# A first product that takes x times g before the norm, and a normed x made while the product runs

## The chip, the cores and the metric

The kernel runs on one core of a Trainium2 chip, as one launch. The core's engines run side by side, each working through its own list of instructions in order: TensorE (PE in the profile; PEld is its load of the stationary operand), VectorE (DVE), ScalarE (ACT), GpSimd (POOL) and SyncE (SP), which issues nearly all transfers. Semaphores join them. The metric is the device time of one execution in microseconds; the time of the kernel before is the median of 3 runs, 882.23 us (881.98 to 883.07).

## The reference

Two layers, each a mixer block and an MLP, on x of 256 tokens by 1024 columns in float32. Only the start of a layer matters here:

```python
def rmsnorm(x, g):
    y = xf * lax.rsqrt(jnp.mean(xf * xf, axis=-1, keepdims=True) + EPS)
    return y * g

for l in range(DEPTH):                       # DEPTH = 2
    h = rmsnorm(x, norm_mix_g[l])
    proj = h @ w_in[l]                       # split: mqk, mv, mo, mi, mf, aq, ak, av, ga, gb
    ...                                      # mLSTM branch, window attention, output projection
    x = x + mixer_block(...)
    x = x + square(relu(rmsnorm(x, norm_mlp_g[l]) @ w_up[l])) @ w_down[l]
return rmsnorm(x, final_norm_g)
```

With r the reciprocal root of a token's mean square, h = (x g) r: r is one number per token (row), g one per column. A product with h's rows can therefore be taken with x g, and each row of the result multiplied by r afterwards.

## The kernel before, in words

**Products in three parts.** A float32 operand is split in a rounded part, hi, and the rest, lo = value - hi. A product is three matmuls: hi with hi, lo with hi, hi with lo (lines L220 to L222 in the helper `xs`, where 128 tokens are the rows of the result; L234 to L236 in `ws`, where the weight's columns are). A weight arrives in pieces of 128x1024 (512 KB) in one of four raw buffers. ScalarE casts the piece to hi (`pump_hi`, L152), VectorE subtracts (`pump_lo`, L127), and the subtraction frees the raw buffer, so the transfer of the piece four further on is issued right behind it, on SP (L89, L108, L109). There are seven pairs of hi and lo.

**Slots.** The program is a list of slots, one for each piece. For each slot are emitted, in this order: what `at` put there; hi of all pieces up to four ahead of the slot's own (`AHEAD`; the table `limits` lowers this at the start); what `at_late` put; lo of the same pieces with the next transfers; what `at_last` put; the slot's matmuls; what `after` put. This is the order of instructions on every engine; nothing moves later.

**The first product.** Slots 0 to 7 ("mv", pieces p0 to p7) compute the values mv: 256 tokens (two token tiles tt of 128) by 1024 columns in two halves hf, so four PSUM banks, each with 8 x 3 matmuls of 128x512, 12 matmuls in a slot, 96 in all. After slot 7 the four banks are copied to the tile vm (ScalarE L605 for hf 0, VectorE L603 for hf 1). Slots 8 to 11 ("kv", p8 to p11) compute the keys kk, values and gates of the attention in three banks that come out of those four; then follow the queries "aq" from slot 12 on. Up to the end all is of this kind.

**The start.** `setup_start` issues the loads: x, the gain row g, the pieces p0 to p3, then eleven small loads (`small_loads`, L393 to L399: gates' biases and sinks spread over 128 partitions, convolution weights), and lets TensorE run 26 + 16 + 8 matmuls on a block of zeros (`N_WARM`, L419, L425, L561). `first_norm` squares x (ScalarE L342, VectorE L344), makes r (VectorE L348, GpSimd L349), multiplies x by r (L534), transposes 128x128 blocks on TensorE (L539) and makes from the PSUM, with the factor g, the parts xh (ScalarE L543, four of 128x128 for half a token tile) and xl (VectorE L549). The first product goes by token tile in slots 0 to 3 (`head="t"`): slots 0 and 1 take tile 0 and the pieces p0 to p3, slots 2 and 3 tile 1; from slot 4 on a slot takes one piece and both tiles. `setup_cols` (slot 4) transposes the convolution rows and the relative bias; `setup_small` (slot 2) fills small constants.

## Time and profile before

| what | us |
|---|---|
| median of 3 runs | 882.23 |
| the profiled execution | 882.83 |
| its span, first to last instruction | 881.1 |
| busy: TensorE, VectorE, ScalarE | 867.6, 566.5, 468.8 |
| first matmul of the first product starts | 8.89 |
| first matmul of slot 5 starts | 27.27 |
| first matmul of the keys (slot 8) starts | 35.74 |
| mean granted clock of TensorE | 0.995 |

Outside the span lie 1.7 us of the profiled execution. Times in the timeline count from the span's start. A row of the timeline has start, length, engine, line, operation, tiles, and in brackets how long the engine had been idle and what released it. In a table by windows the columns are: window and its length, then busy time and number of instructions of PE, PEld, DVE, ACT and POOL, the granted clock (1.00 is full), the share of the DMA engines and GB/s. A group's row gives number, busy time, mean ns of one, and idle time ahead with its releaser. A row of the chain of waits is start, length, and what filled it.

### The profile page before, as it was taken

The numbers are of one execution on the slowest core, as the hardware profiler recorded it, in microseconds if no ns is written. First come the engines' busy times: TensorE is split into PE (matmuls) and PEld (weight loads), VectorE is DVE, ScalarE is ACT, GpSimd is POOL, SyncE is SP. The second block draws the span as 40 slices with busy tenths as digits, with TensorE's granted clock in tenths as the row PEclk, the third lists the DMA queues.
The fourth block names the chain that finished last, engine by engine and source line by source line (L and its number), as shares of the span: only waits on it lengthen the run. The fifth ranks groups of instructions, "written<-read, shape, count | busy, mean of one in ns | idle before, by whom it ended". The sixth has DMA issues, their size and how long they took to land.

```text
span 881.1 us, 15013 instructions
## 1 busy us (share of the span) xinstructions
PE 867.6 (98%) x5929; PEld 792.4 (90%) x5929; DVE 566.5 (64%) x897; ACT 468.8 (53%) x771; POOL 123.1 (14%) x164
## 2 busy tenths in 40 slices
PE   8999999999999999999999999999999999999996
PEld 6899879999989999998889998899998899999985
DVE  5758869666666654546474687776667764737363
ACT  5657866554355554544355567765634453636252
POOL 1361722120000000000001454122000000000000
PEclk9999999999999999999999999999999999999998
DMA  6875445445556737474655453454564466555521
GB/s 217 288 244 190 123 142 164 146 145 163 173 192 209 242 124 253 128 245 128 226 169 192 148 182 109 161 168 144 154 222 158 145 227 222 196 187 188 194 96 48
DMA packets 50711, 155.28 MB, mean 176 GB/s; under 512 B 7912, under 2 KB 10192, under 8 KB 50640
## 3 DMA queue, kind: packets, MB, share of 16 engines
q1 hardware_dynamic: 49456, 150.69, 52.6%
q0 software_dynamic: 896, 3.17, 1.1%
q8 instruction: 46, 0.75, 0.3%
q10 hardware_dynamic: 288, 0.46, 0.1%
q14 instruction: 25, 0.20, 0.1%
HBM read 153.23 MB, written 1.07 MB: 175 GB/s over the span
## 4 chain that ended last, share of the span: by engine, by line
PE 87%; DVE 5%; issue 2%; DMA 2%; ACT 2%; SPq 1%; POOL 1%; POOLq 0%; DVEq 0%; ACTq 0%
PE pa L220 11%; PE pa L221 11%; PE pa L222 11%; PE pa L235 11%; PE pa L234 11%; PE pa L236 11%; PE pb L235 5%; PE pb L234 5%; PE pb L236 5%; DMA raw<-in_w_in 2%; DVE lo L127 2%; PE pb L322 1%; PE pb L860 1%; PE pb L879 1%; PE pb L918 1%
## 5 line engine op out<-in xcount | busy, mean ns | idle before, releaser
L127 DVE TENSOR_TENSOR lo<-raw,hi 128x1024 fp32r<-128x1024 f32 (+1 forms) x276 | 331.5, 1224 | 136.0 <-ACT hi L152 133.5
L152 ACT CAST hi<-raw 128x1024 fp32r<-128x1024 f32 (+1 forms) x280 | 286.1, 1049 | 186.3 <-PE pa L222 49.7
L234 PE MATMUL pa<-xh,hi 128*128 128x256 f32 x864 | 246.6, 285 | 0.0
L235 PE MATMUL pa<-xl,hi 128*128 128x256 f32 x864 | 242.7, 281 | 0.0
L236 PE MATMUL pa<-xh,lo 128*128 128x256 f32 x864 | 241.6, 280 | 0.0
L234 PEld LDWEIGHTS pa<-xh,hi 128*128 128x128 f32 x864 | 162.6, 188 | 1.2 <-ACT vm L605 0.4
L235 PEld LDWEIGHTS pa<-xl,hi 128*128 128x128 f32 x864 | 163.1, 189 | 0.3
L236 PEld LDWEIGHTS pa<-xh,lo 128*128 128x128 f32 x864 | 162.8, 188 | 0.0
L220 PE MATMUL pa<-hi,xh 128*128 128x512 f32 (+1 forms) x384 | 150.5, 392 | 1.5 <-ACT xh L543 1.4
L221 PE MATMUL pa<-lo,xh 128*128 128x512 f32 (+1 forms) x384 | 148.4, 386 | 0.2 <-DVE lo L127 0.2
L222 PE MATMUL pa<-hi,xl 128*128 128x512 f32 (+1 forms) x384 | 148.3, 386 | 0.0
L234 PE MATMUL pb<-xh,hi 128*128 128x256 f32 x384 | 107.6, 280 | 0.0
L235 PE MATMUL pb<-xl,hi 128*128 128x256 f32 x384 | 107.6, 280 | 0.0
L236 PE MATMUL pb<-xh,lo 128*128 128x256 f32 x384 | 107.3, 280 | 0.0
L222 PEld LDWEIGHTS pa<-hi,xl 128*128 128x128 f32 x384 | 72.5, 189 | 15.6
L220 PEld LDWEIGHTS pa<-hi,xh 128*128 128x128 f32 x384 | 72.5, 189 | 14.8 <-ACT xh L543 1.6
L221 PEld LDWEIGHTS pa<-lo,xh 128*128 128x128 f32 x384 | 72.6, 189 | 13.9 <-DVE lo L127 0.6
L349 POOL TENSOR_TENSOR sm<-sm,mhalf 128x1 f32<-128x1 f32 x9 | 6.5, 725 | 499.8 <-DVE sm L348 499.8
L235 PEld LDWEIGHTS pb<-xl,hi 128*128 128x128 f32 x384 | 72.4, 188 | 1.7
L234 PEld LDWEIGHTS pb<-xh,hi 128*128 128x128 f32 x384 | 72.2, 188 | 1.8
L236 PEld LDWEIGHTS pb<-xh,lo 128*128 128x128 f32 x384 | 72.3, 188 | 0.0
L220 PE MATMUL pa<-hi,b 128*128 128x512 f32 x124 | 48.8, 394 | 0.0
(210 smaller groups left out, 979.2 us busy)
## 6 DMA issues: line engine op xcount, KB each, us to landing
raw<-in_w_in SPq DMA_DIRECT2D x104, 512.0 KB, 4.5
raw<-in_w_up SPq DMA_DIRECT2D x64, 512.0 KB, 4.7
raw<-in_w_down SPq DMA_DIRECT2D x64, 512.0 KB, 4.3
raw<-in_w_branch_a SPq DMA_DIRECT2D x16, 512.0 KB, 3.5
raw<-in_w_branch_m SPq DMA_DIRECT2D x16, 512.0 KB, 4.1
raw<-in_w_out SPq DMA_DIRECT2D x16, 512.0 KB, 4.5
b<-ed SPq DMA_DIRECT2D x4, 512.0 KB, 5.4
g<-in_mlstm_norm_g POOLq DMA_DIRECT2D x2, 512.0 KB, 6.1
```

Source lines behind the costliest of these rows:

```text
L127: nc.vector.tensor_tensor(lo[:, :n], raw[:, :n], hi[:, :n].bitcast(F32), op=ALU.subtract)
L152: nc.scalar.copy(hi[:, :n], raw[:, :n])
L220: nc.tensor.matmul(b, xh[:, kt, s], wh[:, c], start=first, stop=False)
L221: nc.tensor.matmul(b, xh[:, kt, s], wl[:, c], start=False, stop=False)
L222: nc.tensor.matmul(b, xl[:, kt, s], wh[:, c], start=False, stop=last)
L234: nc.tensor.matmul(o, wh[:, c], xh[:, kt, :], start=first and half == 0, stop=False, skip_group_check=True)
L235: nc.tensor.matmul(o, wh[:, c], xl[:, kt, :], start=False, stop=False, skip_group_check=True)
L236: nc.tensor.matmul(o, wl[:, c], xh[:, kt, :], start=False, stop=last, skip_group_check=True)
L322: nc.tensor.transpose(pt[:, j * P : (j + 1) * P], src[:, j * P : (j + 1) * P], ident)
L860: nc.tensor.transpose(tp[:, j * P : (j + 1) * P], L[:, j * P : (j + 1) * P], ident)
L879: nc.tensor.matmul(o, va[:, 0, vs], PT[:, 0:T], start=(h < h0 + 2), stop=False, skip_group_check=True)
L918: nc.tensor.matmul(pn[:, :257], W[:, tt * P : (tt + 1) * P], vm[:, 0, h, :], start=True, stop=(tt == 0))
```

## The change

Only the first layer's start is touched. Its parts:

1. **The first product takes x g.** x is transposed as it lands (TensorE L556), with no norm. For chunks 0 to 3 of each token tile hi and lo come straight from PSUM with the factor g (`hi4` ScalarE L570, `lo4` VectorE L576). For chunks 4 to 7 (`rest`, in slots 1 and 2) VectorE first writes x g (`times_g`, L562) and ScalarE and VectorE split it from there (L566, L580); `times_g` is also run for chunks 0 to 3 at the end of slot 1, since x g is needed later.
2. **r is applied when the banks are emptied**: the copies of slot 7 become a scaling by r (ScalarE L656, VectorE L654). The squares are taken in slots 2 and 3.
3. **The normed x for the keys** is made in slots 5 and 6: `rows` has TensorE spread r over partitions (L625, two matmuls) and ScalarE copy it (L628, the tile R); `normed(c)` multiplies four chunks of x g by R (VectorE L633, 128x1024) and splits them (ScalarE L323, VectorE L324).
4. **Order of slots 0 to 3**: by piece (`head="k"`), slot 0's units with hf 0 first, and p0 is loaded, cast (L139) and subtracted (L144) in halves. Limits of hi ahead are 1, 2, 3, 4, 5 for slots 0 to 4.
5. **Loads**: first the left halves of both token tiles, p0 in halves, p1, p2, the right halves, p3; the g row on ScalarE's queue; six small loads, of which a row of biases and sinks is spread by a matmul in `setup_cols` (L460), now in slot 5. `setup_small` moves to slot 8, its two copies to slot 10. `N_WARM` is 22, 6, 14.
6. **The keys take their PSUM bank first**, before the two banks of the values.

```diff
-    N_WARM = (26, 16, 8)
+    N_WARM = (22, 6, 14)
...
+        nc.scalar.dma_start(grow, norm_mix_g[0].rearrange("(k c) -> k c", c=P))
+        for tt in range(2):
+            nc.sync.dma_start(X[:, tt, 0:512], xv[:, tt, 0:512])
+        pump_dma(2)
+        pump_dma()
+        pump_dma()
+        for tt in range(2):
+            nc.sync.dma_start(X[:, tt, 512:], xv[:, tt, 512:])
+        pump_dma()
         small_loads()
...
+        def times_g(tt, hf):
+            nc.vector.tensor_tensor(xg[sl(tt, hf)], pts[tt, hf].rearrange("p (k t) -> p k t", k=4),
+                                    gcol[:, 4 * hf : 4 * hf + 4].unsqueeze(2).to_broadcast([P, 4, P]), op=ALU.mult)
+        def hi4(tt):
+            for j in range(4):
+                nc.scalar.activation(uh[:, j, tt * P : (tt + 1) * P], pts[tt, 0][:, j * P : (j + 1) * P], AF.Copy,
+                                     scale=gcol[:, j : j + 1])
...
+        hi4(0)
+        lo4(0)
+        pump_hi_part(0, 512)
         pump_lo_part(0, 512)
+        hi4(1)
+        lo4(1)
+        pump_hi_part(512, 1024)
         pump_lo_part(512, 1024)
         pump_lo_done()
         pump_hi(0, 1)
         pump_lo()
...
+        u = slots[nxt][0]
+        u[1], u[2] = u[2], u[1]
+        limits[nxt] = 1
+        for i in range(1, 5):
+            limits[nxt + i] = 1 + i
+        for tt in range(2):
+            slots[nxt + 1 + tt][0].insert(2, call(lambda tt=tt: rest(tt)))
+            at_last(nxt + 2 + tt, lambda tt=tt: norm(tt))
...
+        def rows():
+            pr = psB()
+            for tt in range(2):
+                nc.tensor.matmul(pr[:, tt * P : (tt + 1) * P], N[tt].r[:, 0:1].to_broadcast([P, P]), ident, start=True,
+                                 stop=True, skip_group_check=True)
+            S0["R"] = tmp()
+            nc.scalar.copy(S0["R"][:, 0:T], pr[:, 0:T])
+            st["hT"] = xT_tiles(xtag)
+        def normed(c):
+            s = (slice(None), slice(4 * c, 4 * c + 4), slice(None))
+            nc.vector.tensor_tensor(xg[s], xg[s], S0["R"][:, 0:T].unsqueeze(1).to_broadcast([P, 4, T]), op=ALU.mult)
+            evac_split(xg[s], st["hT"][0][s], st["hT"][1][s])
+        at(nxt + 5, rows)
+        at(nxt + 5, lambda: normed(0))
+        at(nxt + 6, lambda: normed(1))
+        for tt in range(2):
+            at_last(nxt + 1, lambda tt=tt: times_g(tt, 0))
...
-        s_mv = xs_group(st, "mv", "hT", w, MV0, head="t")
+        s_mv = xs_group(st, "mv", "hT" if l else "hU", w, MV0, head="t" if l else "k")
...
+            if l == 0:
+                r = S0["r"][tt]()
+                if hf:
+                    nc.vector.tensor_scalar(o, i, r, None, op0=ALU.mult)
+                else:
+                    nc.scalar.activation(o, i, AF.Copy, scale=r)
...
-        at(s_kv, lambda: st.update({("kv", 0): psA(), ("kv", 1): psA(), "kk": psA()}))
+        at(s_kv, lambda: st.update({"kk": psA(), ("kv", 0): psA(), ("kv", 1): psA()}))
...
-            at(s_mv + 2, setup_small)
-            at(s_mv + 4, setup_cols)
+            at(s_mv + 8, setup_small)
+            at(s_mv + 10, setup_copies)
+            at(s_mv + 5, setup_cols)
```

**How the order of instructions moves.** ScalarE, before, from hi of p8 (`hi_397`) to the emptying of the banks and the pieces behind it (`raw`: the piece as loaded, `pa`: a bank):

```order
L152 CAST hi_397<-raw_301 128x1040
L152 CAST hi_423<-raw_346 128x1040
L152 CAST hi_441<-raw_401 128x1040
L152 CAST hi_459<-raw_405 128x1040
L605 COPY vm<-pa_241 128x2x256
L605 COPY vm<-pa_243 128x2x256
```

ScalarE, now, from hi of p5 (`hi_314`): `tmp_370` is R, `xh_372` the hi part of the normed x.

```order
L162 CAST hi_314<-raw_207 128x1024
L628 COPY tmp_370<-pb_367 128x256
L323 CAST xh_372<-b_11_142 128x1024
L162 CAST hi_377<-raw_229 128x1024
L162 CAST hi_380<-raw_257 128x1024
L162 CAST hi_383<-raw_291 128x1040
L162 CAST hi_386<-raw_318 128x1040
L323 CAST xh_372<-b_11_142 128x1024
L162 CAST hi_418<-raw_390 128x1040
L162 CAST hi_436<-raw_394 128x1040
L656 ACTIVATE vm<-pa_209,sm_264 128x2x256
```

R and a cast of the normed x now stand ahead of hi of p6 to p9, and a second cast ahead of hi of p10 and p11 (`hi_436`), which the emptying of the banks follows.

VectorE, now, at the same place, from lo of p5 (`lo_315`); `b_11_142` is x g, then the normed x:

```order
L129 TENSOR_TENSOR lo_315<-raw_207,hi_314 128x1024
L456 COPY cw<-pb_333 128x80
L461 COPY gb_bias<-pb_338 128x16
L462 COPY sink<-pb_338 128x32
L463 TENSOR_SCALAR nsink<-sink 128x32
L465 TENSOR_SCALAR rbT<-pb_336 16x32
L633 TENSOR_TENSOR b_11_142<-b_11_142,tmp_370 128x1024
L324 TENSOR_TENSOR xl_373<-b_11_142,xh_372 128x1024
L129 TENSOR_TENSOR lo_378<-raw_229,hi_377 128x1024
```

In the kernel before, lo of p6 (`lo_392`) to p11 follow one another here with nothing between; now each half of the normed x puts a product and a subtraction between them.

TensorE, now, at the start of slot 5, from the convolution rows' transpose to the slot's first matmuls:

```order
L455 MATMUL pb_333<-ident,b_6_100 128x80
L458 MATMUL pb_336<-ident,rb 16x32
L460 MATMUL pb_338<-b_6_100,ones 128x48
L625 MATMUL pb_367<-ident,sm_264 128x128
L625 MATMUL pb_367<-ident,sm_299 128x128
L230 MATMUL pa_209<-hi_314,xh_140 128x512
```

The spreading of r (L625), on which R waits, stands behind all matmuls of slot 4.

More of the change, by code (lines that the diff above doesn't have):

```diff
@@ L87, in piece, with load @@
     def piece(w, kt, c0):
-        def load(raw):
-            nc.sync.dma_start(raw[:, :1024], w[kt * P : (kt + 1) * P, c0 : c0 + 1024])
+        def load(raw, parts=1):
+            for a in range(0, 1024, 1024 // parts):
+                b = a + 1024 // parts
+                nc.sync.dma_start(raw[:, a:b], w[kt * P : (kt + 1) * P, c0 + a : c0 + b])
         pieces.append((load, 1024))
@@ L117, in pump_dma @@
             raws[j] = wp.tile([P, 1040], F32, tag="raw", bufs=N_RAW, name=nm("raw"))
-            pieces[j][0](raws[j])
+            pieces[j][0](raws[j], *parts)
             n_dma[0] += 1
@@ L129, in pump_lo, with pump_hi_part @@
         los.clear()
+    def pump_hi_part(a, b):
+        j = n_split[0] - (1 if a else 0)
+        if not a:
+            pc[j] = tuple(wp.tile([P, 1040], F32R, tag=t, bufs=N_SPL, name=nm(t)) for t in ("hi", "lo"))
+            los.append(j)
+            n_split[0] += 1
+        nc.scalar.copy(pc[j][0][:, a:b], raws[j][:, a:b])
     def pump_lo_part(a, b):
@@ L416, in setup_start @@
         nc.vector.memset(mask, 0.0)
-        pw = psA()
+        pw = S0["pw"] = psA()
         for _ in range(N_WARM[0]):
             nc.tensor.matmul(pw[:, :P], mask, mask, start=True, stop=True)
-        pg = psA()
-        nc.tensor.transpose(pg[:, :8], grow, ident[:8, :8])
-        S0["gcol"] = const.tile([P, KT], F32, name="gcol")
-        S0["pg"], S0["pw"] = pg, pw
-        for _ in range(N_WARM[1]):
-            nc.tensor.matmul(pw[:, :P], mask, mask, start=True, stop=True)
+        S0["grow"] = grow
     def setup_small():
@@ L443, in setup_cols @@
         nc.vector.tensor_copy(cw, pt[:, :80])
+        ptr = psB()
+        nc.tensor.transpose(ptr[:16, :NB_BUCKETS], S0["rb"], ident[:NB_BUCKETS, :NB_BUCKETS])
         pt = psB()
-        nc.tensor.transpose(pt[:16, :NB_BUCKETS], S0["rb"], ident[:NB_BUCKETS, :NB_BUCKETS])
+        nc.tensor.matmul(pt[:, :48], ones[0:1, 0:1].to_broadcast([1, P]), S0["row"], start=True, stop=True)
+        nc.vector.tensor_copy(gb_bias, pt[:, 0:16].rearrange("p (l c) -> p l c", l=DEPTH))
+        nc.vector.tensor_copy(sink, pt[:, 16:48].rearrange("p (l h) -> p l h", l=DEPTH))
         nc.vector.tensor_scalar(nsink, sink, -1.0, None, op0=ALU.mult)
         rbT = const.tile([16, NB_BUCKETS], F32, name="rbT")
-        nc.vector.tensor_scalar(rbT, pt[:16, :NB_BUCKETS], -1.0, None, op0=ALU.mult)
+        nc.vector.tensor_scalar(rbT, ptr[:16, :NB_BUCKETS], -1.0, None, op0=ALU.mult)
         Et = S0["b8"][:16, 1, 0:384]
@@ L526, in first_norm @@
     def first_norm(st, xtag, nxt):
-        xh, xl = st["hT"] = xT_tiles(xtag)
+        uh, ul = st["hU"] = xT_tiles("xb")
+        xg = big8((P, KT, T))
         N = [Norm(0), Norm(1)]
-        gcol, xn, pts = S0["gcol"], {}, {}
-        def scale(tt, hf):
-            xn[tt, hf] = tmp()
-            nc.vector.tensor_scalar(xn[tt, hf], X[:, tt, hc(hf)], N[tt].r[:, :1], None, op0=ALU.mult)
+        gcol = const.tile([P, KT], F32, name="gcol")
+        pts = {}
         def tr(tt, hf):
@@ L553, in first_norm, with sl @@
-        N[0].square(0)
-        N[0].square(1, "dve")
-        N[0].rstd()
-        nc.scalar.copy(gcol, S0["pg"][:, :8])
-        pump_hi(0, 0)
-        scale(0, 0)
-        tr(0, 0)
-        for _ in range(N_WARM[2]):
-            nc.tensor.matmul(S0["pw"][:, :P], mask, mask, start=True, stop=True)
+                c = hf * 512 + j * P
+                nc.tensor.transpose(pts[tt, hf][:, j * P : (j + 1) * P], X[:, tt, c : c + P], ident)
+        def sl(tt, hf):
+            return (slice(None), slice(4 * hf, 4 * hf + 4), slice(tt * P, (tt + 1) * P))
@@ new lines, in lo4, with lo @@
+        def lo4(tt):
+            for j in range(4):
+                s = (slice(None), j, slice(tt * P, (tt + 1) * P))
+                nc.vector.scalar_tensor_tensor(ul[s], pts[tt, 0][:, j * P : (j + 1) * P], gcol[:, j : j + 1],
+                                               uh[s].bitcast(F32), op0=ALU.mult, op1=ALU.subtract)
+        def lo(tt, hf):
+            nc.vector.tensor_tensor(ul[sl(tt, hf)], xg[sl(tt, hf)], uh[sl(tt, hf)].bitcast(F32), op=ALU.subtract)
+        pg = psA()
+        nc.tensor.transpose(pg[:, :8], S0["grow"], ident[:8, :8])
@@ L562, in first_norm @@
+        nc.vector.tensor_copy(gcol, pg[:, :8])
+        for tt in range(2):
+            tr(tt, 0)
+            for _ in range(N_WARM[1 + tt]):
+                nc.tensor.matmul(S0["pw"][:, :P], mask, mask, start=True, stop=True)
+        hi4(0)
+        lo4(0)
+        pump_hi_part(0, 512)
         pump_lo_part(0, 512)
-        hi(0, (0, 1))
-        lo(0, (0, 1))
+        hi4(1)
+        lo4(1)
+        pump_hi_part(512, 1024)
         pump_lo_part(512, 1024)
@@ L748, in cwc @@
         def cwc(j, m):
[L749 removed]
+            c = 32 * l + j * 8 + m if j < 4 else 64 + 8 * l + m
+            return cw[:, c : c + 1]
         def qk_evac(i):
```

80 lines of the change are left out of this document (29 added, 51 removed).

## The prediction

> **What bounds the kernel now.** I read the page first, its busy shares and the chain that ended last.
>
> ```profile
> span 881.1 us, 15013 instructions
> PE 867.6 (98%) x5929; PEld 792.4 (90%) x5929; DVE 566.5 (64%) x897; ACT 468.8 (53%) x771; POOL 123.1 (14%) x164
> PE 87%; DVE 5%; issue 2%; DMA 2%; ACT 2%; SPq 1%; POOL 1%; POOLq 0%; DVEq 0%; ACTq 0%
> ```
>
> TensorE is busy for 98% of the span, so an edit pays only where TensorE waits, runs at a lower clock, or gets fewer matmuls. The next view is the busy time by stage: the first product, and everything after 80 us.
>
> ```profile
> 8.90:35.70 26.80, 26.27 (x110) 20.33 (x110) 19.88 (x37) 17.47 (x34) 9.94 (x26) 0.94 0.70 237
> 80.00:881.00 801.00, 791.37 (x5394) 722.99 (x5393) 516.08 (x816) 419.44 (x696) 96.74 (x108) 1.00 0.52 170
> ```
>
> After 80 us the change touches nothing but instructions with other operands, so the question is when the keys (slot 8) start and how densely they run. Everything hangs on the first 40 us. The timeline of TensorE there (the matmul at 27.27 opens slot 5, those at 35.74 and 37.13 belong to slot 8):
>
> ```profile
> 8.89 0.77 PE L220 MATMUL pa<-hi,xh 128*128 128x512 f32 x1 [1.43 <-ACT xh L543]
> 9.94 0.63 PE L222 MATMUL pa<-hi,xl 128*128 128x512 f32 x1
> 10.37 0.63 PE L220 MATMUL pa<-hi,xh 128*128 128x512 f32 x1
> 20.15 0.60 PE L539 MATMUL pb<-ident,tmp 128*128 128x128 f32 x4
> 20.51 0.48 PE L220 MATMUL pa<-hi,xh 128*128 128x512 f32 x1
> 20.82 0.40 PE L221 MATMUL pa<-lo,xh 128*128 128x512 f32 x1
> 23.86 0.39 PE L222 MATMUL pa<-hi,xl 128*128 128x512 f32 x1
> 24.09 0.23 PE L442 MATMUL pb<-ident,b 80*128 80x80 f32 x1
> 24.38 0.50 PE L220 MATMUL pa<-hi,xh 128*128 128x512 f32 x1
> 27.27 0.40 PE L220 MATMUL pa<-hi,xh 128*128 128x512 f32 x1
> 35.74 0.39 PE L234 MATMUL pa<-xh,hi 128*128 128x256 f32 x1
> 37.13 0.39 PE L220 MATMUL pa<-hi,xh 128*128 128x264 f32 x1
> ```
>
> A warm 128x512 matmul is issued every 0.234 us (13 from 20.82 to 23.86), a cold one every 0.43 (9.94 to 10.37). The first product's 96 matmuls begin at 8.89; the keys begin at 35.74, and the value matmul of the second token tile, the last that waits for a bank, at 37.13. What releases those two is in the chain of waits:
>
> ```profile
> 29.02 5.02 DMA raw<-in_w_in
> 34.14 1.07 ACT hi L152
> 35.24 0.59 DVE lo L127
> 35.83 0.57 issue
> 36.40 0.69 DVE vm L603
> 37.13 0.39 PE pa L220
> ```
>
> So piece 11 lands at 34.04, ScalarE casts it, VectorE subtracts it, and only then does VectorE empty a bank (L603): TensorE is dense, but ScalarE and VectorE are just in time at the hand-over. That hand-over is where the change adds work.
>
> **What the change saves at the start.** The first matmul no longer waits for squares, rstd, scaling and the transpose of a scaled tile. It needs x transposed, four casts from PSUM, and half of piece 0.
>
> ```profile
> 4.11 0.69 DVE L344 CUSTOM_DVE_ANT_0 tmp<-X 128x512 f32<-128x512 f32 x1 [3.12 <-DMA X<-in_x]
> 7.53 1.04 ACT L152 CAST hi<-raw 128x1024 fp32r<-128x1024 f32 x1 [2.68 <-DMA raw<-in_w_in]
> 15.93 1.14 ACT L543 ACTIVATE xh<-pb,gcol 128x128 fp32r<-128x128 f32 x4 [1.97 <-PE pb L539]
> 17.11 1.12 DVE L549 SCALAR_TENSOR_TENSOR xl<-pb,gcol,xh 128x128 fp32r<-128x128 f32 x4 [0.40 <-ACT xh L543]
> L127 DVE TENSOR_TENSOR lo<-raw,hi 128x1024 fp32r<-128x1024 f32 (+1 forms) x15 | 18.1, 1222 | 8.9 <-ACT hi L152 8.8
> L152 ACT CAST hi<-raw 128x1024 fp32r<-128x1024 f32 (+1 forms) x16 | 16.7, 1057 | 13.1 <-DMA raw<-in_w_in 13.1
> L134 DVE TENSOR_TENSOR lo<-raw,hi 128x512 fp32r<-128x512 f32 x2 | 1.4, 685 | 2.3 <-ACT hi L152 2.3
> L605 ACT COPY vm<-pa 128x512 f32<-128x512 f32 x2 | 1.1, 588 | 0.0
> L603 DVE COPY vm<-pa 128x512 f32<-128x512 f32 x2 | 1.3, 683 | 0.0
> ```
>
> 512 KB of x had landed by 4.1, and the whole of piece 0 by 7.5. The first half of the piece now comes straight behind 512 KB of x, so it lands between 4.1 and 7.5; I take 6.0, just past the middle, because other transfers share the queues. Its cast is half of 1.06 and some fixed part, 0.6 (x's four casts, 1.14, are done before), so the first matmul stands at 6.7, 2.2 earlier. From there:
>
> - Slot 0: 12 matmuls are 2.8. The first lo half takes 0.69 from 6.7, and the second matmul waits 0.5 for it. The second half's lo stands behind four casts (1.14) and a half cast (0.6) on ScalarE and four subtractions (1.12) on VectorE: done about 9.6, where TensorE arrives at 8.8, a wait of 0.8. Slot 1 starts at 10.8.
> - Slots 1 to 4: 48 x 0.234 = 11.2; two groups of four transposes at 0.44 each (0.36 from 20.15 to 20.51, and the next matmul holds 0.31 instead of 0.23) make 0.9; and 0.4 for piece 4's lo, whose engine also multiplies by g four times (0.69 each, by L134). Slot 4 ends at 23.3.
>
> In the kernel before, the same 60 matmuls end at 27.3: 4 us are gained there. Of these, 1.6 are the eight matmuls at half clock (8 x 0.2) that I assume away here; a rival below takes them back.
>
> The small loads were eleven on SP, the queue on which the pieces are issued too, and held piece 4's issue back to 14.69. The two other rows are setup work that moves:
>
> ```profile
> 11.66 0.63 ACT L342 ACTIVATE tmp<-X 128x512 f32<-128x512 f32 x1 [0.17 <-DMA X<-in_x]
> 14.69 2.42 SPq L89 DMA_DIRECT2D raw<-in_w_in  x4
> L434 ACT CAST Rs<-tmp 128x384 fp32r<-128x384 f32 x1 | 0.5, 527 | 0.0
> L428 DVE CAST identb<-ident 128x128 bf16<-128x128 f32 x1 | 0.4, 357 | 0.0
> 20.48 1.05 ACT L152 CAST hi<-raw 128x1024 fp32r<-128x1024 f32 x1 [2.30 <-DMA raw<-in_w_in]
> ```
>
> Now they are six, and piece 4's issue waits for lo of piece 0 (9.6) and for a landing of x, which stands behind about as many bytes as the one at 11.66: 3 us earlier than 14.69. In the sum above this keeps slots 3 and 4 free of a wait over 0.4. The g row goes to ScalarE's queue and needs one issue there, before its first work: nothing. The scaling of the four banks by r replaces copies of 0.59 and 0.68 by operations of the same shape: nothing. The setup copy on ScalarE (0.53) and the cast on VectorE (0.36) move to slots 10 and 8, behind the emptying of the banks, where the next pieces are needed only at slot 12; without that cover, 0.5.
>
> **What it adds at slots 5 and 6.** In the kernel before, the first product and the keys use one normed x. Now the keys alone need it, and it is made on ScalarE and VectorE between their pieces, in the order that the change's rows show. Slot 5 begins with three small matmuls and the two that spread r, about 0.6 by the pair at 24.09 to 24.38 (0.29 for two): they end at 23.9. ScalarE's copy R waits for them. It is queued in front of hi of pieces 6 to 9, and VectorE's product with R in front of lo of the same pieces. Both engines therefore stand still from about 21.5 and 22.7, when piece 5 is done, although pieces 6 and 7 have landed. Then, one after the other:
>
> - R copied, 0.4 (half of L605's shape, with the fixed part): 24.4
> - product of four chunks with R, 128x1024 on VectorE, 1.22 by L127: 25.7
> - cast on ScalarE, 1.06: 26.8; then hi of piece 6, 27.8; VectorE's subtraction 28.0, and lo of piece 6: 29.2
> - lo of pieces 7, 8, 9 at 1.16 back to back (1.22 less the overlap): 32.7
> - second product 33.8, its cast 34.9, hi of pieces 10 and 11 (1.0 each): 36.9
> - ScalarE empties the first bank, 0.6: 37.5. VectorE: subtraction 36.2, lo of 10 and 11: 38.5, its first bank 0.69: 39.2.
>
> TensorE meets this chain three times. Slot 5 takes 23.9 to 26.6; then it waits 1.2 for hi of piece 6 (27.8) and, after one matmul, 1.2 for its lo (29.2). Slots 6 and 7 then end at 34.6. The keys wait until 37.5 (before: 35.74), and the second value matmul, nine short matmuls or 1.1 later, waits from 38.6 to 39.2 (before: 37.13). **Sum: 39.2 - 37.1 = 2.1 us later**, though slot 4 ended 4 us earlier: the 36 matmuls left are 8.4 us of work and the chain beside them 13.6.
>
> Durations that no row of before shows: the product with R, whose second operand repeats over chunks. Its floor is the one-input cast of this shape (1.06), its ceiling twice an operation of 512 columns that reads PSUM (2 x 0.68). I take 1.22: two inputs, both in SBUF, as L127. Two of them stand on the chain: 0.3 down or up. R's copy has half the columns of L605 and lies between 0.3 and 0.6: 0.1 down, 0.2 up. The landing of the first half moves slot 4's end by no more than -0.5 and +0.8, since the waits in slot 0 take up a part. Piece 11 is issued after lo of piece 7 (30.4) and piece 10; with 5.02 as in the chain it lands by 35.9, when ScalarE comes to it; 0.1 later at the ceiling. Together +1.2 to +3.5.
>
> **Rivals.**
> *The gain is kept (faster).* If ScalarE and VectorE had been ahead by the 4 us, the two waits in slot 6 and the one at the keys would be hidden: 23.9 + 8.4 = 32.3, keys 3.4 earlier, and with the bank's emptying 3.1: 879.1. For it: VectorE is busy 19.88 of 26.8 us in that stretch, so there is room in the mean. Against it: the room lies ahead of slot 5, where the rows forbid its use, and the chain above has no free link. It needs the products and casts at half price.
> *Within 0.2%.* Slots 0 to 4 without any wait of theirs: 6.7 + 60 x 0.234 + 0.9 = 21.6, the chain 1.7 earlier, 37.5 against 37.1: +0.4, 882.6. For it: the price of slot 0's waits rests on a landing not seen. Against it: the second half's cast and lo stand behind the second tile's on both engines, wherever the landing falls.
> *Half clock again (slower still).* The granted clock by half microseconds before:
>
> ```profile
> 8.50:9.00 0.50, 0.11 (x1) 0.11 (x1) 0.40 (x1) 0.50 (x4) 0.00 (x0) 0.95 1.00 369
> 9.00:9.50 0.50, 0.50 (x2) 0.31 (x2) 0.50 (x3) 0.50 (x2) 0.00 (x0) 0.50 0.98 369
> 12.00:12.50 0.50, 0.50 (x3) 0.38 (x2) 0.50 (x2) 0.50 (x3) 0.00 (x0) 0.64 0.33 92
> ```
>
> From about 8.95 to 12.35 the clock was half (a tenth of the first row, seven tenths of the last), behind a stretch with gaps of 1.4 and 0.3. The changed start has 42 warm-up matmuls in place of 50 and a gap before the first product of some 0.6, then 0.5 and 0.8 inside slot 0. Eight to twelve matmuls at 0.43 cost 1.6 to 2.4, of which the waits for lo absorb about 1.0: +1.0 on top of the 2.1, 885.3. The Trainium skill ("TensorE: Matmul & The Clock Gate", Part 1: The HAM clock gate) says that free-running windows of about 3.4 us decide, so that one idle window halves the clock for the next; the stretch of 3.4 us above agrees. Its Part 4 (PE-mode transpose) adds that transposes do not count as work there, and the changed start holds eight of them among its warm-ups; no row of this case shows that. By these two the sum would be this rival's.
>
> **How the numbers follow.** A run is told from no change here at about 0.2%, 1.8 us. Forecast (the chain from slot 5 holds the keys): 882.83 + 2.1 = 884.9 for a profiled execution like the one read, which lies 0.6 above the median; for the median 882.23 + 2.1 = 884.3. Its own range, +1.2 to +3.5, is 883.4 to 885.7; chance 0.47, of which 0.38 beyond 884.0. Half clock 885.3: 0.16. Within 0.2%, 882.6: 0.21. Gain kept, 879.1: 0.16. Slower 0.38 + 0.16 = 0.54; same 0.09 + 0.21 = 0.30; faster 0.16. The range reaches down into the unexplained faster cases, to 881.0, and up to 886.7, the half clock (+3.1) with the upper bounds (+1.4).
>
> **What would show it.** In the profile after: first product matmul at 6 to 7.5; slot 5 at 23 to 24.5 with ScalarE and VectorE idle 1 to 3 us ahead of it, released by TensorE; waits of TensorE for hi and lo near 27 and 28 of a microsecond each; a wait of 2 to 3.5 for a bank emptied by ScalarE, keys at 37 to 38. The forecast is wrong if slot 6 starts without a wait, if slot 5 begins after 25, or if the keys start before 36.

## The result, and the profile after

The changed kernel takes 888.57 us (median of 4, 888.23 to 888.97), the kernel before beside it on the same chip 882.57 (881.98 to 883.07): a ratio of 1.007, 95% interval 1.0058 to 1.0082. It is slower, as forecast, but by 6.0 us and not by 2.1, and it lies above the range. In the profiled executions the difference is 5.4 (886.5 against 881.1), and the traces split it so:

| stretch | before | after | difference |
|---|---|---|---|
| start to the second value matmul | 37.13 | 40.33 | +3.2 |
| from there to the last matmul | 835.4 | 836.4 | +1.0 |
| last matmul to the end | 8.57 | 9.80 | +1.2 |

"Last matmul" is the start of the last matmul. The first row is the one that the prediction summed, to 39.2 and not 40.33. The other two have no term in it. The head of the page of the changed kernel:

```profile
span 886.5 us, 15006 instructions
PE 870.3 (98%) x5927; PEld 794.3 (90%) x5927; DVE 571.2 (64%) x896; ACT 470.3 (53%) x770; POOL 121.8 (14%) x165
```

TensorE has two matmuls fewer than before and is busy 2.7 us longer. Its timeline over the first 41 us, cut to the start of the first product, the rows of slot 5's start, and the rows with waits (in brackets the idle time ahead of the row and who ended it):

```profile
7.06 0.48 PE L230 MATMUL pa<-hi,xh 128*128 128x512 f32 x1
7.80 0.50 PE L231 MATMUL pa<-lo,xh 128*128 128x512 f32 x1 [0.27 <-DVE lo L144]
11.59 0.50 PE L231 MATMUL pa<-lo,xh 128*128 128x512 f32 x1 [0.49 <-DVE lo L129]
23.86 0.23 PE L455 MATMUL pb<-ident,b 80*128 80x80 f32 x1
24.06 0.40 PE L460 MATMUL pb<-b,ones 1*128 1x48 f32 x2
24.38 0.71 PE L625 MATMUL pb<-ident,sm 128*128 128x128 f32 x4
24.85 0.48 PE L230 MATMUL pa<-hi,xh 128*128 128x512 f32 x1
28.90 0.50 PE L230 MATMUL pa<-hi,xh 128*128 128x512 f32 x1 [1.03 <-ACT hi L162]
30.35 0.77 PE L231 MATMUL pa<-lo,xh 128*128 128x512 f32 x1 [0.95 <-DVE lo L129]
38.60 0.39 PE L244 MATMUL pa<-xh,hi 128*128 128x256 f32 x1 [1.08 <-ACT vm L656]
40.33 0.39 PE L230 MATMUL pa<-hi,xh 128*128 128x264 f32 x1 [0.38 <-DVE vm L654]
```

Slot 5 opens at 24.85, 2.4 before its 27.27 of the kernel before: the start is faster, and the lead is gone at the keys. Each wait stands where the prediction put it: one each for hi and lo of piece 6, one for ScalarE's bank ahead of the keys, one for VectorE's bank ahead of the second value matmul. Two rows speak of a size that was missed: the one matmul of L460 stands as two records, and the two spreads of r (L625) as four, 24.38 to 24.85. ScalarE's and VectorE's timelines show the chain that the slot hangs on:

```profile
25.19 0.37 ACT L628 COPY tmp<-pb 128x256 f32<-128x256 f32 x1 [3.14 <-PE pb L625]
26.85 1.05 ACT L323 CAST xh<-b 128x1024 fp32r<-128x1024 f32 x1 [1.29 <-DVE b L633]
35.00 1.05 ACT L323 CAST xh<-b 128x1024 fp32r<-128x1024 f32 x1 [3.29 <-DVE b L633]
37.87 1.26 ACT L656 ACTIVATE vm<-pa,sm 128x512 f32<-128x512 f32 x2
```

```profile
25.59 1.23 DVE L633 TENSOR_TENSOR b<-b,tmp 128x1024 f32<-128x1024 f32 x1 [0.53 <-ACT tmp L628]
29.08 4.66 DVE L129 TENSOR_TENSOR lo<-raw,hi 128x1024 fp32r<-128x1024 f32 x4
33.66 1.31 DVE L633 TENSOR_TENSOR b<-b,tmp 128x1024 f32<-128x1024 f32 x1
39.53 1.40 DVE L654 TENSOR_SCALAR vm<-pa,sm 128x512 f32<-128x512 f32 x2
```

ScalarE stands still for 3.14 us until r has been spread, and again for 3.29 until VectorE has made the second half of the normed x behind four subtractions. The chain of waits ends in the same two engines (start, length, what):

```profile
24.45 0.66 PE pb L625 x4
25.19 0.38 ACT tmp L628
25.59 1.24 DVE b L633
26.85 1.06 ACT xh L323
...
33.74 1.24 DVE b L633
35.00 1.06 ACT xh L323
...
39.53 0.75 DVE vm L654
```

The clock was halved too, but not where a rival had it. The table of windows (from the left: window, its length, busy time of TensorE, of its weight loads, of VectorE, ScalarE and GpSimd; then the granted clock):

```profile
8.00:9.00 1.00, 1.00 (x5) 0.82 (x5) 1.00 (x5) 0.61 (x1) 0.00 (x0) 1.00 0.98 381
30.00:30.50 0.50, 0.15 (x1) 0.15 (x2) 0.50 (x2) 0.50 (x1) 0.50 (x2) 0.91 0.00 0
31.00:32.00 1.00, 1.00 (x4) 0.81 (x3) 1.00 (x2) 0.71 (x1) 1.00 (x2) 0.50 0.57 84
33.50:34.00 0.50, 0.50 (x3) 0.44 (x2) 0.50 (x2) 0.00 (x0) 0.50 (x2) 0.68 1.13 374
```

Slot 0 runs at full clock. Behind slot 6's two waits the clock is half from about 30.4 to 33.8. The Trainium skill ("TensorE: Matmul & The Clock Gate", Part 1: The HAM clock gate) gives the window as 3.41 us; the stretch of 3.4 here agrees.

### The profile page after: what moved, and what is told of

Same layout as the page of the kernel before. It is cut to its first block, busy times and chain, and to the rows that moved or that the text cites. A ratio compares the mean times of both kernels' runs of the same rounds, so it can differ in the third digit from the quotient of the medians.

```text
span 886.5 us, 15006 instructions
## 1 busy us (share of the span) xinstructions
PE 870.3 (98%) x5927; PEld 794.3 (90%) x5927; DVE 571.2 (64%) x896; ACT 470.3 (53%) x770; POOL 121.8 (14%) x165
## 4 chain that ended last, share of the span: by engine, by line
PE 86%; DVE 6%; ACT 2%; DMA 2%; issue 2%; POOL 1%; SPq 0%; POOLq 0%; DVEq 0%; ACTq 0%
PE pa L231 12%; PE pa L230 12%; PE pa L232 12%; PE pa L244 9%; PE pa L245 9%; PE pa L246 9%; PE pb L245 5%; PE pb L244 5%; PE pb L246 5%; DVE lo L129 3%; DMA raw<-in_w_in 2%; PE pb L332 1%; PE pb L916 1%; PE pb L935 1%; PE pb L974 1%
```

## The experiments

Theory A is the prediction's own: the keys are late because the normed x is made in a chain behind slot 5's start, on engines that also split the pieces and empty the banks. All times are medians, and each ratio is to the kernel before on the same chip. "Keys to last" is the way from the second value matmul to the last matmul.

| kernel | time | ratio (95%) | second value matmul | keys to last | last to end |
|---|---|---|---|---|---|
| e1, the kernel before once more | 882.32 | 1.0002 (0.9992-1.0011) | 36.51 | 835.3 | 8.57 |
| e2 | 888.44 | 1.0070 (1.0053-1.0087) | 39.53 | 837.3 | 9.71 |
| e3 | 886.76 | 1.0051 (1.0036-1.0066) | 37.96 | 837.5 | 9.80 |
| e4 | 883.62 | 1.0015 (1.0006-1.0024) | 35.15 | 837.9 | 8.73 |
| e5 | 881.69 | 0.9993 (0.9983-1.0002) | 36.73 | 835.0 | 8.48 |
| e6 | 888.42 | 1.0069 (1.0054-1.0084) | 39.23 | 837.9 | 9.86 |
| e7 | 885.55 | 1.0039 (1.0026-1.0053) | 36.88 | 836.3 | 9.87 |
| e8 | 883.60 | 1.0015 (1.0006-1.0025) | 34.64 | 837.7 | 8.83 |
| e9 | 881.01 | 0.9985 (0.9976-0.9994) | 37.18 | 834.6 | 8.59 |
| e10 | 887.96 | 1.0066 (1.0053-1.0078) | 39.56 | 836.8 | 9.80 |
| e11 | 881.83 | 0.9998 (0.9989-1.0007) | 33.83 | 837.0 | 9.86 |
| e12 | 881.91 | 0.9996 (0.9987-1.0005) | 36.58 | 835.5 | 8.57 |
| e13 | 886.24 | 1.0048 (1.0035-1.0060) | 39.56 | 835.9 | 9.79 |
| e14 | 884.54 | 1.0031 (1.0020-1.0042) | 36.86 | 837.5 | 8.59 |
| e15 | 879.91 | 0.9974 (0.9964-0.9984) | 33.55 | 835.7 | 9.76 |

**e1**, without an edit, gives the spread of what is compared.

> The kernel before, unchanged, to see how far two executions of one kernel differ outside the first 41 us. In the two profiles so far the changed kernel is 3.2 us later at the second value matmul (37.13 to 40.33), another 1.0 later at its last matmul (872.5 to 876.7) and another 1.2 at the span's end (881.1 to 886.5). Theory A (all of the loss that belongs to the change lies before 41 us, the rest varies from execution to execution): this profile has its last matmul at 872.5 +- 0.5, and the time from there to the span's end differs from the first profile's 8.6 by up to 1. Theory B (the rest belongs to the changed kernel): last matmul and end within 0.2 of the first profile. Time within 0.3 of 882.6 in both.

Its second value matmul came 0.6 earlier than in the first profile of the same kernel, at the same pace behind it and with the same end: the 1.0 and the 1.2 belong to the changed kernel, as theory B has it. Differences of half a microsecond at the keys say nothing, then; over the first profile, e1, e5 and e9, kernels with the same instructions on TensorE, the second value matmul lies between 36.51 and 37.18.

**e2** fills TensorE's waits in slot 6, so that its clock stays full there.

```diff
+        def filler(n):
+            pf = psB()
+            for _ in range(n):
+                nc.tensor.matmul(pf[:, :P], mask, mask, start=True, stop=True)
+
+        slots[nxt + 6][0].insert(0, call(lambda: filler(16)))
```

> The changed kernel with 16 warm-up matmuls on the block of zeros ahead of slot 6's first matmul, which fill the wait of 1.2 us for hi of piece 6 and keep TensorE busy. Theory A (the chain on ScalarE and VectorE from R on sets when the keys start; the waits of slot 6 and the half clock from 30.5 to 33.8 are covered by it): the clock stays full or halves later, slot 7 ends up to 1.7 earlier, the keys start at 38.6 and the second value matmul at 40.3 as without, time 888.6 +- 0.5. Rival (the half clock after the waits costs its 1.7 us): keys 1.7 earlier, 886.9.

```profile
31.00:34.00 3.00, 3.00 (x14) 2.46 (x14) 3.00 (x3) 0.00 (x0) 2.68 (x4) 1.00 1.09 309
34.00:37.00 3.00, 1.11 (x5) 0.56 (x3) 1.89 (x3) 2.80 (x3) 1.25 (x6) 1.00 0.93 341
39.00:42.00 3.00, 2.82 (x13) 2.51 (x13) 3.00 (x5) 1.83 (x4) 0.00 (x0) 0.50 0.84 281
```

Slots 6 and 7 run at full clock now, and TensorE only waits the longer in front of the keys (1.11 us of work in 34 to 37). The half clock of slot 6 was hidden behind the chain: the rival's 886.9 is refuted by 888.44. The second value matmul comes 0.8 earlier than in the changed kernel, which A did not say; R's copy begins 0.8 earlier too (24.40 and not 25.19), so the chain from there is as long as before. What is more, behind the longer wait the clock is half from 39 to 42, on the keys, where it costs: this is the 1.0 that "keys to last" is above the changed kernel's. In e3, e6 and e10 too the half clock lies somewhere between 37 and 42.

**e3** brings the splits of pieces 6 and 7 forward into slot 4, so that they stand ahead of R and the first half of the normed x.

```diff
+        limits[nxt + 3], limits[nxt + 4] = 5, 7
```

> The changed kernel with hi and lo of piece 6 in slot 3's and of pieces 6 and 7 in slot 4's limits (5 and 7 in place of 4 and 5), so that they stand ahead of R on ScalarE and VectorE, in time in which both stood still. Theory A (the chain): two lo of 1.16 leave the chain, R's product may start up to 1 us later; second value matmul at 38.9 to 39.3, time 887.3 +- 0.5. Rival (waits of slot 6 and the half clock behind them are the loss): both vanish, 2.0 + 1.7, so 884.9.

The time is 1.8 below the changed kernel's; A's figure was 887.3, the rival's 884.9. The waits of slot 6 are gone, and TensorE waits 3.1 us ahead of the keys instead, with the half clock behind it. So the order on ScalarE and VectorE in those slots has a price, as A says, but only a part of the loss.

**e4** leaves out the chain; keys and all later products of this mixer then lack the factor r, so only its time is of use.

```diff
-        uh, ul = st["hU"] = xT_tiles("xb")
+        uh, ul = st["hU"] = xT_tiles(xtag)
...
-        at(nxt + 5, rows)
-        at(nxt + 5, lambda: normed(0))
-        at(nxt + 6, lambda: normed(1))
+        st["hT"] = st["hU"]
```

> The changed kernel without the normed x: rows() and normed() are left out, keys and all later products of layer 1's mixer take x times g (this leaves out the norm's factor there). It measures what making the normed x costs in all. Theory A: chain without R, two products, two casts, two subtractions (4.9 on VectorE, part of which it waits anyway): second value matmul at 35.4 to 36.2 in place of 40.33, time 884.0 +- 0.7. Rival (its work fits beside the pieces, and only its place ahead of piece 6 costs): no more than 3.7, so 884.9 or more.

Without R, the products and their casts the second value matmul comes at 35.15, 5.2 before the changed kernel and 2.0 before the kernel before (A: 35.4 to 36.2, and 884.0 for the time): the chain is what eats the lead. And yet the kernel ends later than the one before. Here "keys to last" is 837.9 against 835.4, and with e1 this says that something behind the keys slows down that has nothing to do with the chain.

**e5 and e6** test a first guess at it, that one new small constant shifts every buffer behind it by 32 bytes: e5 adds such a constant to the kernel before, e6 takes it out of the changed one.

```diff
(e5)
+        pad = const.tile([P, 4], F32, name="pad")
+        nc.gpsimd.memset(pad, 0.0)
(e6)
-        z2 = S0["z2"] = const.tile([P, 4], F32, name="z2")
+        z2 = S0["z2"] = small()[:, 0:4]
```

> The kernel before with one more constant of 16 bytes per partition (and one memset of it on GpSimd), as the changed kernel has one: it moves every tile allocated behind it (raw buffers, hi, lo, x parts, temporaries) up by 32 bytes and changes nothing else. From the keys to the end the changed kernel without the normed x lost 2.5 us against the kernel before, evenly: 128x256 matmuls are issued every 118.2 ns in place of 117.8, in two executions of the kernel before alike. Theory P (where the tiles lie sets that pace): pace 118.2 ns, loss 2.5, time 884.7 +- 0.5. Rival (the pace has another cause): 882.2 +- 0.4.

> The changed kernel with that 16-byte constant taken from the rotating small buffers, so that all tiles but the two pairs of x parts and what lies behind them are where the kernel before has them. The first 41 us stay as they are. Theory P: the 1.0 us that the changed kernel loses evenly between the keys and the end goes back, 887.5 +- 0.4. Rival: 888.5 +- 0.4.

Neither time moves (881.69 beside 882.31, 888.42 beside 888.57). The guess is refuted from both sides.

But e6, the changed kernel but for those 32 bytes, comes to the same time by another way. Three matmuls of its timeline (the start of slot 5, of the keys, and the second value matmul), and two windows:

```profile
23.75 0.48 PE L230 MATMUL pa<-hi,xh 128*128 128x512 f32 x1
37.51 0.38 PE L244 MATMUL pa<-xh,hi 128*128 128x256 f32 x1 [2.70 <-ACT vm L656]
39.23 0.59 PE L230 MATMUL pa<-hi,xh 128*128 128x264 f32 x1
```

```profile
38.00:40.00 2.00, 2.00 (x11) 1.90 (x10) 2.00 (x5) 1.57 (x3) 0.00 (x0) 0.50 0.86 274
40.00:42.00 2.00, 2.00 (x14) 2.00 (x13) 2.00 (x2) 1.26 (x4) 0.00 (x0) 0.65 0.78 283
```

Slot 5 opens 1.1 us earlier than in the changed kernel's profile, and the second value matmul comes 1.1 earlier, at the forecast's 39.2. The waits of slot 6 are the same (1.04 and 0.96), yet the clock stays full there. It is half on the keys instead, until about 41.4, which by this costs about 1.1, an estimate from half of the 2.2 us behind 39.23. The 3.2 us of the first table's first row are therefore one profile's figure: some 1.1 of them can stand ahead of the second value matmul or, as a half clock, behind it.

**e7** empties the first product's four banks ahead of the splits of pieces 10 and 11.

```diff
-        z2 = S0["z2"] = const.tile([P, 4], F32, name="z2")
+        z2 = S0["z2"] = small()[:, 0:4]
+        limits[nxt + 6] = 9
+        limits[nxt + 7] = 9
```

> The changed kernel (tiles as in the run without the shift) with the limits of slots 6 and 7 at piece 9, so that hi and lo of pieces 10 and 11 stand behind the emptying of the banks. Theory A (the chain on ScalarE and VectorE holds the keys): two casts of 1.0 and two subtractions of 1.16 leave the chain, second value matmul 2.2 earlier (38.1), time 2.2 below the run without the shift, 885.3 if that is 887.5. Rival (TensorE's own waits and the half clock): no change from it.

2.9 us less than e6, which differs by the two limits alone. The second value matmul comes 2.35 earlier than in e6 (A: 2.2); besides, TensorE waits only 0.8 ahead of the keys, and no half clock falls on them. The banks are indeed queued behind splits that only the next slots need; A holds.

**e8** moves the normed x ahead: norms one slot earlier, R at slot 4, both products on GpSimd, the casts behind slots 5 and 6, and e3's and e7's limits.

```diff
+        def scaled(c):
+            ...
+            (nc.gpsimd, nc.gpsimd)[c].tensor_tensor(xg[s], xg[s], S0["R"][:, 0:T].unsqueeze(1).to_broadcast([P, 4, T]),
+                                                      op=ALU.mult)
...
+        at(nxt + 4, rows)
+        at(nxt + 4, lambda: scaled(0))
+        at(nxt + 4, lambda: scaled(1))
+        at_last(nxt + 5, lambda: normed(0))
+        at_last(nxt + 6, lambda: normed(1))
```

> The changed kernel with the normed x off the chain: limits 5, 7, 9, 9 for slots 3, 4, 6 and 7, squares of x in slots 1 and 2, r spread in slot 4, the two products with R on GpSimd, the splits at the end of slots 5 and 6; tiles as in the run without the shift. Theory A: the keys start when slot 7 ends, second value matmul at 34.0 +- 0.6 in place of 40.3; time 6.3 below the run without the shift, 881.2 +- 0.8, below the kernel before if the end is as there. Rival (something besides the chain keeps the changed kernel back): 883 or more.

The second value matmul stands at 34.64, where A had it (34.0 within 0.6); the time is 2.4 above A's 881.2 and fits the rival. Rows of its timelines, of VectorE, GpSimd and ScalarE, tell a part of why:

```profile
22.23 6.49 DVE L129 TENSOR_TENSOR lo<-raw,hi 128x1024 fp32r<-128x1024 f32 x2 [0.19 <-ACT hi L162]
```

```profile
21.33 6.31 POOL L637 TENSOR_TENSOR b<-b,tmp 128x1024 f32<-128x1024 f32 x2 [3.25 <-ACT tmp L632]
33.93 6.85 POOL L474 COPY b<-rbT 16x3 f32<-16x3 f32 x16
```

```profile
43.26 0.51 ACT L450 CAST Rs<-tmp 128x384 fp32r<-128x384 f32 x1 [5.78 <-POOL sm L444]
```

While GpSimd multiplies for 6.3 us, two subtractions on VectorE take 6.49, which elsewhere take 1.22 each. GpSimd's setup work moves back behind its products, ScalarE waits 5.78 for it, and TensorE waits 0.36 and 0.49 at 46 to 48. Matmul by matmul beside the kernel before, e8 loses 1.4 us by 60 us; another 1.0 goes evenly up to the end, of which e13 to e15 speak. The Trainium skill ("GPSIMD Engine Reference", 1. Specifications) says that GpSimd shares its way into SBUF with VectorE and gets in the way of VectorE's operations with two SBUF inputs; the two subtractions of 6.49 here are such operations, and agree.

**e9 and e10** test where the normed x lies. Buffers are laid out in the order of their first use, and the change uses `xb` first.

```diff
(e9, in the kernel before)
+        xT_tiles("xb")
+        tmp()
         xh, xl = st["hT"] = xT_tiles(xtag)
(e10, in the changed kernel)
+        xT_tiles(xtag)
         uh, ul = st["hU"] = xT_tiles("xb")
```

> The kernel before, with one thing of the change alone: the buffer pair xb is claimed ahead of xa, as the change does by using xb for x times g. The pool lays buffers out in the order of their first use, so the normed x (pair xa, an operand of nearly every matmul of the projections) moves from byte 161,504 of each partition to byte 186,080, as in the changed kernel; no instruction is added, removed or moved. Theory L (where the normed x lies sets the even pace of the matmuls): the interval of a 128x256 matmul goes from 0.1176 to 0.1182 us between 250 and 450 us, the way from the second value matmul to the last matmul from 835.35 to about 836.4 us, the time from 882.3 to 883.4. Rival (the pace comes from the banks, from the loads or from anything else of the change): 0.1176, 835.35, and 882.3 within 0.3. The last store, which lands 1.2 us later after its matmul in the changed kernel than before, tells apart in the same way: 9.8 us from last matmul to the end if it follows the layout, 8.5 if not.

> The changed kernel with that one thing undone: xa is claimed ahead of xb, so the normed x lies at byte 161,536 again (32 bytes from where it was before; a shift of 32 bytes alone changed nothing). Theory L: a 128x256 matmul every 0.1176 us instead of 0.1182, second value matmul still at 40.3, from there to the last matmul 835.4 instead of 836.35, time 888.5 - 1.0 = 887.5 (886.3 if the last store follows the layout too). Rival: 0.1182, 836.35, 888.5.

Theory L is refuted by its sign: the kernel before gets 1.3 us *faster* with the layout of the changed one (881.01, interval 0.9976 to 0.9994), and the changed kernel keeps its pace with the layout of the one before. But e9 also shows that a layout alone, without one instruction moved, is worth about a microsecond (1.3 by the medians, of which 0.7 between the second value matmul and the last in the traces).

**e11** is e8 with the products on VectorE, behind slot 4's own work, and with e10's line. **e12** is e7's two limits in the kernel before.

```diff
(e11, against e8)
-            (nc.gpsimd, nc.gpsimd)[c].tensor_tensor(...)
+            (nc.vector, nc.vector)[c].tensor_tensor(...)
-        at(nxt + 4, lambda: scaled(0))
-        at(nxt + 4, lambda: scaled(1))
+        at_last(nxt + 4, lambda: scaled(0))
+        at_last(nxt + 4, lambda: scaled(1))
(e12, against the kernel before)
+        limits[nxt + 6] = limits[nxt + 7] = 9
```

> The changed kernel with four edits: the two norms one slot earlier, the spread of r at the start of slot 4, the two products of 1.2 us each on VectorE behind slot 4's own work, splits of the normed x behind slots 5 and 6, and the four banks emptied ahead of the splits that only the slots after need; and xa claimed first, as in the run beside it. Theory A (the keys are late because the normed x is made in a chain behind slot 5's start, and because the banks are emptied behind splits): TensorE goes from slot 0 to the keys with no wait over 0.6 us, second value matmul at about 34.0 (33.5 to 34.8), 6.3 before the changed kernel and 3.1 before the kernel before. Theory A with theory L: 882.3 - 3.1 = 879.2 (878.6 to 880.2). A without L: 880.2. Rival (as in the run with GpSimd's products, what is gained at the keys is given back at the next stage, because VectorE's or ScalarE's queue is late there): 882 to 883.6.

> The kernel before with one edit: in slots 6 and 7 the splits of pieces 9 to 11 are held back until the first product's four banks have been emptied (two limits of 9). Theory A (the keys wait for banks that stand behind splits in ScalarE's and VectorE's queues, in the kernel before too): the wait of 1.2 us ahead of the keys goes, second value matmul at about 35.2 instead of 37.1, time 882.3 - 1.9 = 880.4. Rival (the wait is only passed on to the split pieces that the keys and the queries use): second value matmul at 35.2 but waits for hi or lo of 1 to 2 us in the keys or just behind them, 882.3 within 0.5.

In e11 TensorE has no wait from slot 5 to the keys, and the second value matmul comes at 33.83: A's 34.0. Of the 3.3 us to the first profile of the kernel before, 2.9 are lost again by the end: 0.6 until 87 us, about 1.0 by the pace and 1.3 behind the last matmul. In e12 the wait ahead of the keys is gone, and yet the second value matmul comes at 36.58: 0.55 before that of the first profile, and not before the 36.51 of e1, whose slot 4 ended 1.1 earlier (the transpose behind it at 22.88, in e12 at 24.00) and which then waited 0.60 at the keys. So no gain is shown; A's 1.9 was too much, and 881.91 is not told from 882.33.

**e13, e14 and e15** test what the traces of all these kernels have in common. Put matmul by matmul beside the buffers, the mean time from one issue to the next of the matmuls with 256 columns shows one step that differs:

```
mean ns from a matmul's issue to the next one's, by the weights of both
                         before    e9    e14   after   e10    e13    e11    e15
hi (of xh) -> hi (of xl)  118.4  118.5  118.5  118.6  118.6  118.5  118.5  118.5
hi (of xl) -> lo          118.3  118.2  118.3  118.0  118.0  118.1  118.0  118.2
lo -> hi                  116.7  116.3  117.9  117.7  117.7  116.5  117.7  116.3
(some 1130 to 1240 of each, from 45 us to the end)
```

Piece j's hi and lo lie in one of seven buffers each. In the kernel before both go through the numbers 0 6 5 4 3 2 1. In the changed kernel hi goes 0 6 5 4 1 2 3 and lo 0 6 5 1 2 3 4, and so on to the end: this is read from the addresses in the two programs. The step from lo to hi is 117.6 to 117.9 in every kernel with the change but e13 and e15. It fits a pool that gives out what came free first, since the new start frees them in another order. e13 (in the changed kernel) and e15 (in e11 without e10's line) fix the order of the kernel before; e14 gives that of the change to the kernel before.

```diff
+    ORDER = {"hi": [0, 6, 5, 4, 3, 2, 1], "lo": [0, 6, 5, 4, 3, 2, 1]}
+
+    def spl(t, j):
+        return wp.tile([P, 1040], F32R, tag=t + str(ORDER[t][j % N_SPL]), bufs=1, name=nm(t))
...
-            hi = wp.tile([P, 1040], F32R, tag="hi", bufs=N_SPL, name=nm("hi"))
-            lo = wp.tile([P, 1040], F32R, tag="lo", bufs=N_SPL, name=nm("lo"))
+            hi = spl("hi", j)
+            lo = spl("lo", j)
```

> The changed kernel with the seven buffers of hi and of lo claimed in a fixed order, the one of the kernel before (piece j gets hi and lo of the same number, 0 6 5 4 3 2 1); nothing else is moved. In the changed kernel the pool gives hi 0 6 5 4 1 2 3 and lo 0 6 5 1 2 3 4. Theory H (the pairing of hi and lo buffers sets the pace): the step from a matmul on lo to the next on hi takes 116.3 to 116.7 ns instead of 117.65, some 1130 times, so 1.1 to 1.5 us less between the second value matmul and the last matmul (836.35 to about 835.1), time 888.5 - 1.3 = 887.2 (886.2 to 887.5, the lower end if the normed x's place now helps as in e9). Rival (the pace comes from the PSUM banks or from the work of other engines): 117.65, 836.35, 888.5.

> The kernel before with the order of the hi and lo buffers of the changed kernel (hi 0 6 5 4 1 2 3, lo 0 6 5 1 2 3 4), nothing else moved. Theory H: the step from lo to hi goes from 116.7 to about 117.65 ns, the way from the second value matmul to the last matmul from 835.35 to about 836.4, time 882.3 + 1.05 = 883.4 (883.0 to 883.8). Rival: 116.7, 835.35, 882.3.

> The kernel of e11 with the normed x left where the changed kernel has it, and the hi and lo buffers in the order of the kernel before. Theory H: second value matmul at 33.8 as in e11, from there to the last matmul 1.1 to 1.8 us less than the 837.0 of e11, and the end behind the last matmul 8.5 to 9.9 us as the store falls; time 881.8 - 1.1 to 881.8 - 1.8, about 880.3 (879.0 to 880.8), so faster than the kernel before (882.3). Rival: 881.8.

Theory H holds in all three, and the columns e13, e14 and e15 of the table above show the step itself going back and forth. e13 takes 886.24, 2.3 less than the changed kernel; matmul by matmul it gains 1.95 from 43 us to the end, and loses 1.5 between the second value matmul and there, because the clock, half in slot 6 as before, was half a second time on the keys:

```profile
40.00:44.00 4.00, 4.00 (x23) 4.00 (x22) 3.79 (x5) 2.49 (x5) 0.00 (x0) 0.58 0.85 273
```

e14 costs the kernel before 2.4 us (884.54), more than the 1.05 expected: the step from lo to hi gives 1130 x 1.2 ns = 1.4, and the matmuls with 512 columns slow down as well. Its 837.5 from the keys to the last matmul is close to the 837.9 of e4, which has the same place of the normed x and the same order of buffers. e15 beats both kernels: 879.91, 0.26% under the kernel before (interval 0.16 to 0.36%) and 8.7 us under the changed one. Its windows at the place where the changed kernel waits show no wait and full clock:

```profile
core 0 of [0], span 879.0 us
...
28.00:32.00 4.00, 4.00 (x19) 3.24 (x18) 4.00 (x5) 2.67 (x4) 4.00 (x1) 1.00 0.79 235
32.00:36.00 4.00, 4.00 (x33) 3.90 (x32) 3.84 (x5) 3.96 (x5) 4.00 (x17) 1.00 0.36 111
```

**Behind the last matmul** no experiment was made; the traces alone speak. The last store (out<-b) is issued 4.76 us after the last matmul everywhere. It lands 2.8 us later in the kernel before, 3.5 in the changed one, 2.5 in e8 (rows of the DMA view of the three kernels, in this order):

```profile
out<-b SPq DMA_DIRECT2D x1, 320.0 KB, 2.8
```

```profile
out<-b SPq DMA_DIRECT2D x1, 320.0 KB, 3.5
```

```profile
out<-b SPq DMA_DIRECT2D x1, 320.0 KB, 2.5
```

Around it falls one 8-KB packet of the queue that fetches instructions:

```
us after the last matmul      fetch begins  store's last packet done  end
before, e1, e5, e9, e12, e14  6.93 - 7.04   6.93 - 7.05               8.5 - 8.6
after, e2, e3, e6, e7, e10,
  e11, e13, e15               6.81 - 6.98   7.40 - 7.69               9.7 - 9.9
e4, e8                        8.4, 8.6      6.85, 6.93                8.7, 8.8
```

Where the fetch begins just ahead of the store's last packets, these end 0.4 to 0.8 later; where it comes behind, they do not. The rest is SyncE: it waits for its DMA semaphores one by one, and the last store's is its last but two in the kernel before (0.95 from its landing to the end) and stands ahead of five others in the changed one (1.52). This accounts for the 1.2, in all seventeen traces in the same way, but no run moved the fetch by itself: that it delays the store is read from the times, not shown.

## Why the prediction was right and wrong

- **The start.** First product at 7.06 (6.7 forecast), waits of 0.27 and 0.49 in slots 0 and 1 (0.5 and 0.8, both in slot 0), no half clock there: right in the main, and the rival of a half clock at slots 0 and 1 fell.
- **"Slots 1 to 4 end 23.3", "about 0.6" for the small matmuls and the spread of r.** Slot 4 ended at 23.86, 0.6 late, and from there to the end of R's copy it took 1.7 and not 1.1, the small matmuls standing as more records than were counted. R was copied at 25.57 and not 24.4. Only the second half is a mis-sized term: e6 has it too (22.77 to 24.46). The first follows a landing: the cast of piece 2 waited for its transfer until 10.48 here and until 9.39 in e6, where slot 4 ended 0.5 before the forecast. That e6 meets 24.4 and 39.2 is luck, one error against the other. Of the signs named, slot 5 (24.85), the wait for ScalarE's bank (1.08) and the keys (38.60) fell outside in the changed kernel's profile; in e6's all three fall inside (23.75, 2.70, 37.51).
- **The chain from R to the second value matmul.** Right almost to the tenth: 14.8 forecast (24.4 to 39.2), 14.76 measured (25.57 to 40.33). The order of the operations, their prices by the rows of the kernel before, and the place where it ends all held, and e3, e4, e7 and e11 move it the way its mechanism says. TensorE's wait ahead of the keys was 1.08 and not 2.9, since the half clock in slot 6 made TensorE late as well; that cost nothing (e2). Where the wait is 2.7 (e2, e6, e10) the half clock falls on the keys, and there it does cost; the sum has no term for a half clock behind its own waits.
- **"After 80 us the change touches nothing but instructions with other operands."** This is the step that failed. It is true of the instructions, and the conclusion drawn from it, that the sum may stop at the keys, is wrong. The other operands are other buffers: the pairing of hi and lo costs about 2 us from the keys to the last matmul (1.95 in e13, 2.1 in e14), and +1.0 is left of it. That the new place of x gives back the rest fits e9, but e10 did not show it. Behind the last matmul +1.2 came with the store. 3.2 + 1.0 + 1.2 is the 5.4 of the profiles. The last 0.6 to the medians is that the profile of the kernel before lies 0.3 above its median here and that of the changed kernel 0.3 below.
- **The rivals.** "Gain kept" needs what e11 and e15 do: the normed x out of the pieces' way. "Within 0.2%" asked for slots 0 to 4 without waits: in e6 TensorE has none there over 0.15 us, and R is copied at 24.46 all the same, not 1.7 before the forecast's 24.4.

What is open: why the step from lo to hi depends on which buffers are paired; why the place of x helps in e9 and seems to do nothing in e10; which edit of the change sets off the other order of buffers (e4, without the normed x, has the step of 117.9 too); where the half clock falls; and whether the fetch of instructions is what delays the last store.

## What to carry to other kernels

When an operation is moved onto engines that also feed the critical one, cost its whole queue, link by link, up to the next hand-over: this gave 14.8 for 14.76. Where a change alters the order in which buffers are claimed or freed, compare the addresses in the rest of the program with those before: with 98% of the span on TensorE, 1 ns on one step in three is a microsecond. And a sum that ends at the hand-over needs a bound for the rest and for the tail, not a zero.

## What the runs showed of the hardware

- The issue interval of back-to-back matmuls depends on which SBUF buffers the weights come from: the step from lo to hi of the same shape goes from 117.7 to 116.5 ns in the changed kernel (e13) and from 116.7 to 117.9 in the kernel before (e14) by the pairing of buffers alone.
- Behind two waits of one microsecond, one matmul of 0.50 us apart, the clock was half for 3.4 us in the changed kernel (the windows from 30 to 34). But the same two waits stand in e6 and e7, and the clock stays full behind them. Where the halving falls moves by microseconds from kernel to kernel: on slot 6 in the changed one, on the keys in e2, e3, e6 and e10, on both in e13, nowhere in e7, although e6 differs from the changed kernel by 32 bytes only.
- VectorE's subtraction of two SBUF operands took 2.7 times as long beside a product on GpSimd (6.49 for two, 2.4 elsewhere), and one of 1.23 took 2.29 beside GpSimd's later work (e8). The two ended at 25.37 and 28.72, each 1.1 after the end of a GpSimd product (24.29, 27.64), about the time of a subtraction by itself. By these times the work moved to GpSimd ran in turns with VectorE's, not beside it.
